# Key norms, group mean and key selection of a hybrid decoder step: three edits in one

## The chip, the cores and the metric

The kernel runs on one core of one Trainium2 chip. The metric is the device time of one execution in microseconds (us), the median of several runs. The engines of the core work in parallel, each through its own queue in order: TensorE (PE; its weight loads, PEld, overlap its matmuls), VectorE (DVE), ScalarE (ACT), GpSimd (POOL) and SyncE (SP), which issues the transfers. Matmuls write their results to PSUM, from where DVE and ACT read them.

## What is computed

One inference step of a two-layer decoder. The tokens are a prompt of 1,024 and eight sample sequences of eight tokens. Layer 0 mixes by RWKV-7 (a recurrence over a 64 x 64 state per head, 16 heads), layer 1 by sparse attention in which an indexer selects 256 keys per query; each mixer is followed by a feed-forward block (1,024 to 4,096 to 1,024). The lines of the reference that the change touches:

```python
kk = hd(k * P['rw_k_k'][j]).astype(F32)
kk = kk * lax.rsqrt(jnp.maximum(jnp.sum(kk * kk, axis=-1, keepdims=True), 1e-24))   # per token and head of 64
k = k * (1 + (a - 1) * P['rw_k_a'][j])
S, y = wkv7_scan(S0, hd(r), hd(decay), hd(k), hd(v), -kk, kk * hd(a).astype(F32))
mu = jnp.mean(y, axis=-1, keepdims=True)
var = jnp.mean(jnp.square(y - mu), axis=-1, keepdims=True)
y = ((y - mu) * lax.rsqrt(var + GN_EPS)).reshape(B, T, D)
...
adm = pos_k[None, None, :] <= pos_q[None, :, None]
_, idx = lax.top_k(jnp.where(adm, score, -jnp.inf), topk)      # topk = 256
```

## The kernel before

The tokens are worked through in two groups: A holds the 64 sample tokens and prompt tokens 0 to 511 (five token tiles, 576 columns), B holds prompt tokens 512 to 1,023 (four tiles, 512 columns). Activations lie transposed, with channels on the partitions. Large matmuls keep 32-bit accuracy by splitting weights and activations into a high and a low part (`mm3`, L133: three matmuls per block; `split`, L143; `loadw`, L113, whose high part is a cast on ScalarE).

The order in which a Python program issues the work is a priority only: when the program is built, a planner simulates the engines and lays down one fixed order per engine, in which work issued later fills the places that earlier work would leave idle, as long as its buffers are free. `RATES` (L75) says how often a step of the side work is issued between steps of the main work; where it is 0, the side work is issued after it and only fills gaps.

The stages: `rwkv_proj` (L543) of half A, with the adaLN weights streamed in beside it; the recurrence `wkv` (L945), with the projections of half B and then the output projection and feed-forward block of half A as filler; `dsa_proj` (L1002); sparse attention of A (`att_mixed`, L1359) with layer 0's feed-forward block of B as filler; sparse attention of B (`att_prompt`, L1338) with layer 1's feed-forward block of A; then what is left of A's block, and B's.

`rwkv_proj` makes six tensors; the last loop (L582 on) makes r, k and v, eight blocks of 128 channels each, and stores each block to the scratch tensor R. Its results leave PSUM through `mmt` tiles (tag o, four banks).

The recurrence is cut into 34 units (16 of half A's prompt, two of the sample group, 16 of half B), each of 256 columns: two channel blocks (a block holds two heads) by 128 tokens, or for the sample group four blocks by 64. Each unit has four parts, `prep`, `inv1`, `inv2` and `rec`; in round t the program issues, step by step in turn, `rec` of unit t-3, `inv2` of t-2, `inv1` of t-1 and `prep` of t. `prep` reads r, k, w, a, v from R, takes the key norm (`sq`, then `tokrsqrt`: matmuls that sum over the 64 channels of a head into `nps`, then `rsqrt`, L158, on 128 x 4 numbers, then matmuls that spread the root over the channels into `rb`) and makes the operands of the recurrence. `rec` runs the two chunks of 64 tokens, then the group norm of the output: mean `mu`, difference `yc`, square, and `tokrsqrt` again. All PSUM tiles of `prep` but one share one bank (tag p, `psp`), all of `rec` one other bank (tag r, `psr`), those of the inversions two (`psi`). `rsqrt` is a bit trick and three Newton steps: 11 DVE instructions in a row.

`topk` (L1171) finds the 256th largest score of each row bit by bit, from bit 30 down to bit 0 of a threshold: at each bit a candidate is made, the scores at or above it are counted, and the bit is kept or not. Bits 30 to 16 are counted on bf16 copies `tu` of the scores, the others on the scores themselves. It runs four times: in att_mixed for two prompt tiles together (384 and 512 columns) and for the 64 sample rows (2,056 columns), in att_prompt for two pairs of tiles (640 and 768, 896 and 1,024 columns).

## Time and profile before

| | us |
|---|---|
| median of three runs | 4378.32 |
| lowest and highest run | 4348.06, 4389.85 |
| profiled execution | 4376.47 |
| its span, first to last instruction | 4374.7 |
| PE busy (share) | 4008.7 (92%) |
| DVE busy | 2647.1 (61%) |
| ACT busy | 1681.9 (38%) |
| POOL busy | 971.5 (22%) |

All rows come from that one profiled execution. Busy time is time in which an instruction of the engine was running; a wait is the idle time in front of an instruction, put down to the instruction whose result came last. The granted clock is TensorE's, as a share of its higher level: 1.0 is 2.4 GHz all the time, 0.5 is 1.2 GHz all the time.

### The profile page before, as it was taken

How to read it: one execution, taken by the hardware profiler on the slowest of the kernel's cores; microseconds unless marked ns; L12 is line 12 of the kernel's file. 1: busy time of each engine (PE TensorE's matmuls, PEld its weight loads, DVE VectorE, ACT ScalarE, POOL GpSimd, SP SyncE). 2: the span in 40 equal slices, each digit the busy share in tenths (PEclk: the TensorE clock that was granted, in tenths of full speed). 3: DMA queues.
4: the chain of work that ended last, by engine and by line, in shares of the span. 5: the costliest groups of instructions: out<-in, count | busy, mean ns of one | idle time of the engine just before them, and what ended most of it. 6: DMA issues, size and time to landing. Idle time of an engine off the chain costs nothing. (4 is left out here: it accounts for less than half of the span.)

```text
span 4374.7 us, 77889 instructions
## 1 busy us (share of the span) xinstructions
PE 4008.7 (92%) x31096; PEld 3205.7 (73%) x31096; DVE 2647.1 (61%) x6822; ACT 1681.9 (38%) x3169; POOL 971.5 (22%) x762
## 2 busy tenths in 40 slices
PE   7997899998999999989899888989778999999999
PEld 5796566666777799988655565778667667998887
DVE  5513766565677655552887964442899965555444
ACT  5533544443345333332444333332443333333333
POOL 1321222222333222211111122222110000222222
PEclk7797779998798999998899999998879999999999
DMA  6675222333221122234332145444211111322332
GB/s 224 211 237 183 66 65 78 99 89 95 59 56 51 45 80 82 78 114 140 102 84 67 53 153 193 141 128 151 69 50 41 40 39 34 116 87 90 96 96 87
DMA packets 506749, 433.94 MB, mean 99 GB/s; under 512 B 93777, under 2 KB 451777, under 8 KB 501202
## 3 DMA queue, kind: packets, MB, share of 16 engines
q1 hardware_dynamic: 500498, 391.20, 30.2%
q0 software_dynamic: 5888, 37.75, 2.5%
q8 instruction: 245, 4.01, 0.4%
q14 instruction: 118, 0.97, 0.1%
HBM read 360.48 MB, written 67.87 MB: 98 GB/s over the span
## 5 line engine op out<-in xcount | busy, mean ns | idle before, releaser
L126 POOL TENSOR_TENSOR wl<-w,wh 128x1024 fp32r<-128x1024 f32 (+1 forms) x258 | 615.8, 2391 | 2330.8 <-ACT wh L122 2076.9
L140 PE MATMUL o<-hi,wh 128*128 128x512 f32 (+4 forms) x2592 | 891.8, 347 | 27.3 <-ACT hi L144 23.6
L140 PE MATMUL o<-lo,wh 128*128 128x512 f32 (+4 forms) x2592 | 890.7, 345 | 18.4 <-DVE lo L145 14.1
L140 PE MATMUL o<-hi,wl 128*128 128x512 f32 (+4 forms) x2592 | 886.3, 343 | 2.5 <-DVE wl L126 2.3
L122 ACT CAST wh<-w 128x1024 fp32r<-128x1024 f32 (+3 forms) x388 | 396.4, 1035 | 985.8 <-PE o L140 816.0
L388 DVE SCALAR_TENSOR_TENSOR xr<-o,mods,xr 128x256 f32<-128x256 f32 (+1 forms) x816 | 463.3, 570 | 292.9 <-PE o L140 281.0
L140 PEld LDWEIGHTS o<-hi,wh 128*128 128x128 f32 (+1 forms) x2592 | 499.2, 194 | 86.6 <-ACT hi L144 28.8
L140 PE MATMUL o<-uh,wh 128*128 128x320 f32 (+2 forms) x1536 | 522.1, 340 | 41.5 <-DVE xr L388 33.0
L140 PEld LDWEIGHTS o<-lo,wh 128*128 128x128 f32 (+1 forms) x2592 | 500.2, 193 | 74.2 <-DVE lo L145 20.1
L140 PEld LDWEIGHTS o<-hi,wl 128*128 128x128 f32 (+1 forms) x2592 | 499.1, 193 | 50.8 <-issue 10.0
L140 PE MATMUL o<-uh,wl 128*128 128x320 f32 (+2 forms) x1536 | 515.3, 336 | 1.8 <-POOL wl L126 1.1
L140 PE MATMUL o<-ul,wh 128*128 128x320 f32 (+2 forms) x1536 | 516.7, 336 | 0.0
L140 PEld LDWEIGHTS o<-uh,wh 128*128 128x128 f32 x1536 | 294.3, 192 | 80.3 <-DVE xr L388 41.0
L140 PEld LDWEIGHTS o<-uh,wl 128*128 128x128 f32 x1536 | 294.2, 192 | 29.8 <-issue 5.7
L140 PEld LDWEIGHTS o<-ul,wh 128*128 128x128 f32 x1536 | 294.7, 192 | 28.0 <-issue 5.8
L126 DVE TENSOR_TENSOR wl<-w,wh 128x1024 fp32r<-128x1024 f32 (+2 forms) x130 | 183.6, 1412 | 216.5 <-ACT wh L122 212.1
L145 DVE TENSOR_TENSOR ul<-z,uh 128x512 fp32r<-128x512 f32 (+1 forms) x128 | 128.5, 1004 | 164.2 <-ACT uh L144 164.1
L1018 PE MATMUL o<-wl,hi 128*128 128x256 f32 (+2 forms) x648 | 188.1, 292 | 6.9 <-POOL wl L126 6.9
L1018 PE MATMUL o<-wh,hi 128*128 128x256 f32 (+2 forms) x648 | 187.1, 291 | 6.9 <-ACT hi L144 6.9
L1018 PE MATMUL o<-wh,lo 128*128 128x256 f32 (+2 forms) x648 | 183.9, 291 | 0.0
L1268 ACT ACTIVATE sm<-sm,st 128x128 f32<-128x128 f32 (+7 forms) x128 | 99.3, 776 | 139.4 <-DVE st L1267 83.8
L1018 PEld LDWEIGHTS o<-wl,hi 128*128 128x128 f32 (+1 forms) x648 | 126.8, 196 | 9.1 <-POOL wl L126 9.1
(411 smaller groups left out, 7063.1 us busy)
## 6 DMA issues: line engine op xcount, KB each, us to landing
w<-in_w_up SPq DMA_DIRECT2D x128, 512.0 KB
w<-in_w_down SPq DMA_DIRECT2D x128, 512.0 KB
wa<-in_w_ada SPq DMA_DIRECT2D x96, 512.0 KB
w<-in_rw_w_rkv SPq DMA_DIRECT2D x48, 512.0 KB
w<-in_att_w_in SPq DMA_DIRECT2D x32, 512.0 KB
RA<-pt SPq DMA_DIRECT2D x48, 288.0 KB
RB<-pt SPq DMA_DIRECT2D x48, 256.0 KB
in<-RA SPq DMA_DIRECT2D x32, 320.0 KB
```

Of the source, the lines that this page charges most:

```text
L122: nc.scalar.copy(h[:kp, :n], w[:kp, :n])
L126: eng.tensor_tensor(out=l[:kp, :n], in0=w[:kp, :n], in1=h[:kp, :n], op=ALU.subtract)
L140: nc.tensor.matmul(o[0:M, 0:c1 - c0], a, b[:, c0:c1], start=(i == 0 and q == 0), stop=(i == n - 1 and q == 2))
L145: (lo_eng or self.nc.vector).tensor_tensor(out=lo, in0=src, in1=hi, op=ALU.subtract)
L388: nc.vector.scalar_tensor_tensor(out=xm[:, p0:c1], in0=o[:, p0 - c0:c1 - c0], scalar=self.mods[l][:, j * 8 + m, 8:9], in1=xm[:, p0:c1], op ...
L1018: nc.tensor.matmul(o[0:n, 0:cw], a, w, start=(k == 0 and q == 0), stop=(k == 7 and q == 2))
L1268: nc.scalar.activation(out=sm[:, 0:L], in_=sm[:, 0:L], func=AF.Exp, scale=-1.0, bias=mn[:, 0:1], accum_out=sums)
```

## The change

The key norm: after each block of k is stored, `rwkv_proj` squares the block (scaled by `rw_k_k`) on ScalarE, sums over each head with one matmul per token tile against a two-column selector `hsel`, and takes the maximum with 1e-24 into a small tile `kn` (128 tokens x tiles x 16 heads) that stays on the chip. After the eighth block one `rsqrt` over the whole tile (80 columns for A, 64 for B) replaces it by its root. `prep` only spreads the root of its tokens and heads into `rb`; its square, sums, maximum, `rsqrt` and one `yield` are gone. Instead of the tile that held the square, `bo` reuses `tk`.

The group mean: the matrix of `mu` is now identity minus the mean (`cent`), so its product is the difference itself; it is copied out of PSUM on ScalarE instead of being subtracted on DVE.

The selection: candidate and kept threshold are one word `cf`. Each bit is set ahead; after the count, `no` is minus the bit where the bit must be cleared, and one instruction clears it and sets the next. The bf16 copies are gone, and every count reads the 32-bit scores.

```diff
@@ -157,6 +157,9 @@
 
     def rsqrt(self, pool, x, P, n, name):
         nc = self.nc
+        if pool is None:
+            class pool:
+                tile = staticmethod(lambda shape, dt, name, tag, bufs=1: self.tmp(name, dt)[:, 0:shape[1]])
         t = pool.tile([128, n], I32, name=name + "i", tag=name + "i")
         nc.vector.tensor_scalar(out=t[:P], in0=x.bitcast(I32), scalar1=1, scalar2=None, op0=ALU.logical_shift_right)
         y = pool.tile([128, n], F32, name=name + "y", tag=name + "y", bufs=2)
@@ -181,6 +184,12 @@
         self.const = const
         self.onec = cp.tile([128, 2], F32, name="onec")
         nc.vector.memset(self.onec, 1.0)
+
+        self.hsel = cp.tile([128, 2], F32, name="hsel")
+        nc.vector.memset(self.hsel, 0.0)
+        for h in range(2):
+            nc.vector.memset(self.hsel[h * 64:h * 64 + 64, h:h + 1], 1.0)
+        self.kn = {}
 
     def vectors(self):
         nc, I, cp = self.nc, self.I, self.cp
@@ -543,6 +552,7 @@
     def rwkv_proj(self, g, h):
         nc, W, I = self.nc, g.W, self.I
         R = self.rscr(g)
+        self.kn[g.name] = self.cp.tile([128, len(g.tiles), 16], F32, name="kn" + g.name)
 
         for n, w1, w2, rk, slot in ((1, "rw_w1", "rw_w2", 64, 2), (4, "rw_a1", "rw_a2", 64, 3), (5, "rw_g1", "rw_g2", 160, 5)):
             xs = self.mixed(g, h, n)
@@ -588,6 +598,25 @@
                 self.mm3(g, [(hw[:, k * 128:k * 128 + 128], lw[:, k * 128:k * 128 + 128]) for k in range(8)], xs,
                          lambda o, c0, c1: nc.scalar.copy(t[:, c0:c1], o[:, 0:c1 - c0]))
                 nc.sync.dma_start(R[m, :, slot, 0:W], t[:, 0:W])
+                if i == 1:
+
+                    if m == 0:
+                        ss = self.kn[g.name]
+                        if g.ns:
+                            nc.vector.memset(ss[:, 0], 1.0)
+                    sq = self.tmp("ks")
+                    nc.scalar.activation(out=sq[:, 0:W], in_=t[:, 0:W], func=AF.Square, scale=self.rv["kk"][:, m:m + 1])
+                    o = self.mmt()
+                    for it, (c0, n_, _, _) in enumerate(g.tiles):
+                        nc.tensor.matmul(o[0:n_, it * 2:it * 2 + 2], sq[:, c0:c0 + n_], self.hsel, start=True, stop=True)
+                    nt = len(g.tiles)
+                    for i0, i1, P in ((0, 1, 64), (1, nt, 128)) if g.ns else ((0, nt, 128),):
+                        nc.vector.tensor_scalar(out=ss[0:P, i0:i1, m * 2:m * 2 + 2], in0=o[0:P, i0 * 2:i1 * 2].rearrange("p (i h) -> p i h", h=2),
+                                                scalar1=1e-24, scalar2=None, op0=ALU.max)
+                    if m == 7:
+                        sv = ss.rearrange("p i h -> p (i h)")
+                        y = self.rsqrt(None, sv, 128, nt * 16, "kn")
+                        nc.vector.tensor_copy(sv, y)
 
 
     def wkv_state(self):
@@ -629,23 +658,12 @@
         pps = lambda nm: self.psp.tile([128, 512], F32, name=nm, tag="p")
         ips = lambda nm: self.psi.tile([128, 512], F32, name=nm, tag="i")
 
-        def tokrsqrt(src, nm, scale, eps, mx, ps_):
-
-            ps = ps_("nps")
-            for i in range(2):
-                nc.tensor.matmul(ps[:, i * 2:i * 2 + 2], src[:, i * 128:i * 128 + 128], self.hsel, start=True, stop=True)
-            ss = T1(nm + "s", [128, 4])
-            if mx:
-                nc.vector.tensor_scalar(out=ss, in0=ps[:, 0:4], scalar1=1e-24, scalar2=None, op0=ALU.max)
-            else:
-                nc.vector.tensor_scalar(out=ss, in0=ps[:, 0:4], scalar1=scale, scalar2=eps, op0=ALU.mult, op1=ALU.add)
-            y = self.rsqrt(l1, ss, 128, 4, nm)
-            rb = ps_("rb")
-            for i in range(2):
+        def spread(y, n, ps):
+
+            for i in range(256 // n):
                 for h in range(2):
-                    nc.tensor.matmul(rb[half(h), i * 128:i * 128 + 128], y[:, i * 2 + h:i * 2 + h + 1].to_broadcast([128, 64]),
-                                     self.ident, start=True, stop=True)
-            return rb[:, 0:256]
+                    nc.tensor.matmul(ps[half(h), i * n:i * n + n], y(i)[:, h:h + 1].to_broadcast([n, 64]), self.ident[0:n, 0:n], start=True, stop=True)
+            return ps[:, 0:256]
 
         def prep():
             R = self.scr["R" + g.name]
@@ -662,11 +680,8 @@
             nc.scalar.activation(out=et(1, L + 1), in_=bst(cum), func=AF.Exp, scale=CDEC)
             Ei = T1("Ei", [128, 256])
             nc.scalar.activation(out=Ei, in_=cum, func=AF.Exp, scale=-CDEC)
-            sq = T1("sq", [128, 256])
-            for i, p in enumerate(pairs):
-                nc.scalar.activation(out=pcol(sq, i), in_=pcol(k, i), func=AF.Square, scale=rv("kk", p))
-            yield
-            rb = tokrsqrt(sq, "kn", None, None, True, pps)
+            ti = c0 // 128 if not g.ns else 0 if sam else 1 + (c0 - g.ns) // 128
+            rb = spread(lambda i: self.kn[g.name][0:tw, ti, pairs[i] * 2:pairs[i] * 2 + 2], tw, pps("rb"))
             tk = T1("tk", [128, 256])
             for i, p in enumerate(pairs):
                 nc.scalar.activation(out=pcol(tk, i), in_=pcol(a, i), func=AF.Identity, scale=rv("ka", p), bias=self.ka1[:, p:p + 1])
@@ -710,7 +725,7 @@
                 EL = X["EL"] = T3("EL", [128, 4])
                 nc.gpsimd.tensor_copy(EL, E[:, :, L])
                 nc.gpsimd.tensor_tensor(out=BH, in0=BK[:, :, 0:2], in1=EL.unsqueeze(2).unsqueeze(3).to_broadcast([128, 4, 2, 64]), op=ALU.mult)
-            bo = T1("bo", [128, 256], tag="sq")
+            bo = tk
             for i, p in enumerate(pairs):
                 nc.vector.scalar_tensor_tensor(out=pcol(bo, i), in0=pcol(r, i), scalar=rv("rk", p), in1=pcol(tk, i), op0=ALU.mult, op1=ALU.mult)
 
@@ -923,12 +938,18 @@
                     yield
 
             mu = rps("mu")
-            nc.tensor.matmul(mu[:, 0:256], self.bones, y, start=True, stop=True)
+            nc.tensor.matmul(mu[:, 0:256], self.cent, y, start=True, stop=True)
             yc = T1("yc", [128, 256])
-            nc.vector.scalar_tensor_tensor(out=yc, in0=mu[:, 0:256], scalar=-1.0 / 64, in1=y, op0=ALU.mult, op1=ALU.add)
+            nc.scalar.copy(yc, mu[:, 0:256])
             nc.scalar.activation(out=y, in_=yc, func=AF.Square)
             yield
-            rb = tokrsqrt(y, "gn", 1.0 / 64, 64e-5, False, rps)
+            ps = rps("nps")
+            for i in range(2):
+                nc.tensor.matmul(ps[:, i * 2:i * 2 + 2], y[:, i * 128:i * 128 + 128], self.hsel, start=True, stop=True)
+            ss = T1("gns", [128, 4])
+            nc.vector.tensor_scalar(out=ss, in0=ps[:, 0:4], scalar1=1.0 / 64, scalar2=64e-5, op0=ALU.mult, op1=ALU.add)
+            gy = self.rsqrt(l1, ss, 128, 4, "gn")
+            rb = spread(lambda i: gy[:, i * 2:i * 2 + 2], 128, rps("rb"))
             nc.vector.tensor_tensor(out=yc, in0=yc, in1=rb, op=ALU.mult)
             for i, p in enumerate(pairs):
                 nc.scalar.activation(out=pcol(yc, i), in_=pcol(yc, i), func=AF.Identity, scale=rv("lnw", p), bias=rv("lnb", p))
@@ -953,7 +974,9 @@
         self.bones = const("c_bones", [128, 128])
         self.smask = const("c_smask", [128, 8])
         self.rmask = const("c_rmask", [128, 2, 256], F16)
-        self.hsel = self.bones[:, 0:128:64]
+
+        self.cent = ltp.tile([128, 128], F32, name="cent")
+        self.nc.vector.scalar_tensor_tensor(out=self.cent, in0=self.bones, scalar=-1.0 / 64, in1=self.ident, op0=ALU.mult, op1=ALU.add)
 
         self.identh = ltp.tile([128, 64], F32, name="identh")
         for h in range(2):
@@ -1177,39 +1200,30 @@
             return pp.tile(shape, dt, name=nm, tag=tag, bufs=bufs)
         Lm = max(s.shape[1] for s in scs)
         cnt = T1("cnt", [128, n])[0:R]
-        m = T1("tm", [128, n], I32)[0:R]
-        cand = T1("tcand", [128, n], I32)[0:R]
         cf = T1("tcf", [128, n], I32)[0:R]
-        xm = T1("txm", [128, n], I32)[0:R]
-        ok = T1("tok", [128, n], I32)[0:R]
+        no = T1("tno", [128, n], I32)[0:R]
         junk = T1("tj", [128, Lm], BF16)[0:R]
 
-        ups = []
-        for i, s in enumerate(scs):
-            u = T1("tu%d" % i, [128, Lm], BF16)[0:R, 0:s.shape[1]]
-            nc.vector.tensor_copy(u, s.bitcast(BF16).rearrange("p (l b) -> p l b", b=2)[:, :, 1])
-            ups.append(u)
-        yield
-
-        def count(th, op, src):
-            for i, s in enumerate(src):
+        def count(th, op):
+            for i, s in enumerate(scs):
                 L = s.shape[1]
                 nc.vector.tensor_scalar(out=junk[:, 0:L], in0=s, scalar1=th if isinstance(th, float) else th[:, i:i + 1], scalar2=None,
                                         op0=op, op1=ALU.add, accum_out=cnt[:, i:i + 1])
-        count(0.0, ALU.is_ge, scs)
-        nc.vector.tensor_scalar(out=xm, in0=cnt, scalar1=float(TOPK) - 0.5, scalar2=-1.0, op0=ALU.is_lt, op1=ALU.mult)
-        nc.vector.memset(m, 0)
+        count(0.0, ALU.is_ge)
+
+        nc.vector.tensor_scalar(out=no, in0=cnt, scalar1=float(TOPK) - 0.5, scalar2=-1.0, op0=ALU.is_lt, op1=ALU.mult)
+        nc.vector.tensor_scalar(out=cf, in0=no, scalar1=1 << 30, scalar2=None, op0=ALU.bitwise_xor)
+        th = cf.bitcast(F32)
         yield
         for b in range(30, -1, -1):
-            nc.vector.tensor_scalar(out=cand, in0=m, scalar1=1 << b, scalar2=None, op0=ALU.bitwise_or)
-            nc.vector.tensor_tensor(out=cf, in0=cand, in1=xm, op=ALU.bitwise_xor)
-            count(cf.bitcast(F32), ALU.is_ge, ups if b >= 16 else scs)
-            nc.vector.tensor_scalar(out=ok, in0=cnt, scalar1=float(TOPK) - 0.5, scalar2=None, op0=ALU.is_ge)
-            nc.vector.copy_predicated(m, ok, cand)
-            yield
-        nc.vector.tensor_tensor(out=cf, in0=m, in1=xm, op=ALU.bitwise_xor)
-        th = cf.bitcast(F32)
-        count(th, ALU.is_gt, scs)
+            count(th, ALU.is_ge)
+            nc.vector.tensor_scalar(out=no, in0=cnt, scalar1=float(TOPK) - 0.5, scalar2=float(1 << b), op0=ALU.is_lt, op1=ALU.mult)
+            if b:
+                nc.vector.scalar_tensor_tensor(out=cf, in0=no, scalar=1 << (b - 1), in1=cf, op0=ALU.bitwise_xor, op1=ALU.bitwise_xor)
+            else:
+                nc.vector.tensor_tensor(out=cf, in0=no, in1=cf, op=ALU.bitwise_xor)
+            yield
+        count(th, ALU.is_gt)
         yield
         for i, s in enumerate(scs):
             L = s.shape[1]
@@ -1403,7 +1417,7 @@
                 p2, p3 = P("attt", 1, c1), P("attsi", 1, c1)
                 ssc = p3.tile([64, LS], F32, name="ssc")
                 tiles = [None] + [self.att_tile(g, i, p2, S[i], 512) for i in range(1, 5)]
-                smp = [self.sample_index(p3, ssc, gather, ki_rows, csm), self.topk(p3, [ssc], 64, {"tj": ("kis", 1), "tu0": ("rls", 1), "teq": ("kiraw", 2), "trk": ("kiraw", 2)},
+                smp = [self.sample_index(p3, ssc, gather, ki_rows, csm), self.topk(p3, [ssc], 64, {"tj": ("kis", 1), "teq": ("kiraw", 2), "trk": ("kiraw", 2)},
                                                                                                    lambda s: [s[:, a * 1024:a * 1024 + 1024].rearrange("r (b c) -> r c b", b=2)[:, c0:c0 + 256]
                                                                                                               for a in range(2) for c0 in (0, 256)] + [s[:, PAST:LS].unsqueeze(2)])]
                 self.together(RATES["tile1A"], [self.topk(p2, S[3:5], place={"teq": ("sm", 3), "trk": ("sm", 3)})], tiles[1:3], smp[0:1])
```

## Rows read from the trace of the kernel before

**Rows 1.** The page: busy us (share of the span) and instructions of each engine.

```profile
PE 4008.7 (92%) x31096; PEld 3205.7 (73%) x31096; DVE 2647.1 (61%) x6822; ACT 1681.9 (38%) x3169; POOL 971.5 (22%) x762
```

**Rows 2.** By stage: start:end us, length, PE, PEld, DVE, ACT, POOL busy, clock, DMA.

```profile
0.00:392.00 392.00, 354.06 (x2594) 286.88 (x2594) 148.40 (x300) 172.52 (x326) 91.41 (x53) 0.85 0.73 229
392.00:1040.00 648.00, 589.45 (x5836) 402.67 (x5834) 408.44 (x1181) 296.99 (x653) 172.68 (x208) 0.83 0.30 83
1040.00:1570.00 530.00, 497.50 (x6624) 398.58 (x6625) 364.94 (x1251) 220.68 (x533) 164.20 (x204) 0.89 0.20 56
...
2180.00:2540.00 360.00, 323.94 (x1561) 205.39 (x1561) 312.38 (x820) 145.72 (x321) 57.07 (x33) 0.94 0.25 69
...
3080.00:3520.00 440.00, 370.88 (x2159) 292.40 (x2157) 402.79 (x1164) 157.11 (x299) 42.62 (x19) 0.86 0.17 50
```

**Rows 3.** Waits of PE, 392 to 1570: line, releaser, total us, times, longest.

```profile
PE spn L918 <- DVE S L912: 8.1, 12, 2.0
...
PE rb L646 <- DVE kny L170: 6.1, 5, 2.5
...
PE nps L636 <- DVE BT L728: 4.0, 4, 2.0
...
PE bb L732 <- DVE UV L728: 0.6, 1, 0.6
```

**Rows 4.** Waits of PE on DVE, first and last: 2180 to 2540, then 3080 to 3520.

```profile
PE o L140 <- DVE xr L388: 9.2, 2, 8.6
PE sp L1169 <- DVE tok L1207: 5.3, 3, 2.7
...
PE il L1440 <- DVE kis L1435: 0.2, 1, 0.2
...
PE pt L1285 <- DVE PT L1287: 12.4, 9, 4.9
...
PE sp L1169 <- DVE ql L1163: 0.4, 1, 0.4
```

**Rows 5.** Timeline of PE: start us, length, line, output, inputs, count.

```profile
498.61 0.61 PE L636 MATMUL nps<-c_bones,sq 128*128 128x2 f32 x4
...
528.35 0.61 PE L636 MATMUL nps<-c_bones,y 128*128 128x2 f32 x4
...
531.40 0.61 PE L636 MATMUL nps<-c_bones,sq 128*128 128x2 f32 x4
...
535.01 0.66 PE L646 MATMUL rb<-c_ident,gny 128*64 128x128 f32 x8 [0.79 <-DVE gny L170]
...
537.39 1.11 PE L646 MATMUL rb<-c_ident,kny 128*64 128x128 f32 x6
```

**Rows 6.** Groups of instructions, whole span: count, busy us, mean ns, idle before.

```profile
L170 DVE SCALAR_TENSOR_TENSOR kny<-knb,kny 128x4 f32<-128x4 f32 x102 | 26.3, 258 | 1.6
...
L636 PE MATMUL nps<-c_bones,sq 128*128 128x2 f32 x136 | 22.2, 265 | 4.1 <-DVE BT L728 4.0
...
L257 ACT COPY adas<-oa 128x256 f32<-128x256 f32 x48 | 17.9, 373 | 45.8 <-PE oa L255 45.8
...
L928 DVE SCALAR_TENSOR_TENSOR yc<-mu,y 128x256 f32<-128x256 f32 x34 | 14.4, 424 | 21.5 <-PE mu L926 19.9 <-PE o L140 1.5
```

**Rows 7.** Timeline of DVE in the selection of half B, one bit.

```profile
3271.45 0.17 DVE L1207 TENSOR_SCALAR tok<-cnt 128x2 int32<-128x2 f32 x1
...
3272.25 0.88 DVE L1197 TENSOR_SCALAR_CACHE_REDUCE tj<-sc,tcf 128x640 bf16<-128x640 f32 x1
```

**Rows 8.** The selection's counts by form: shortest, middle and longest ns.

```profile
L1197 DVE TENSOR_SCALAR_CACHE_REDUCE tj<-tu,tcf x105: 579/1005/2346, 2196.6 to 3409.1; 128x384 bf16<-128x384 bf16 x15, 128x512 bf16<-128x512 bf16 x15, 64x2056 bf16<-64x2056 bf16 x15, 128x640 bf16<-128x640 bf16 x15
...
L1197 DVE TENSOR_SCALAR_CACHE_REDUCE tj<-sc,tcf x102: 598/944/1280, 2252.8 to 3510.7; 128x384 bf16<-128x384 f32 x17, 128x512 bf16<-128x512 f32 x17, 128x640 bf16<-128x640 f32 x17, 128x768 bf16<-128x768 f32 x17
...
L1197 DVE TENSOR_SCALAR_CACHE_REDUCE tj<-ssc,tcf x17: 2335/2346/2349, 2457.7 to 2524.9; 64x2056 bf16<-64x2056 f32 x17
```

**Rows 9.** Waits of ACT, 392 to 1570.

```profile
ACT wh L122 <- PE o L140: 46.1, 30, 8.9
```

## Prediction, made before the changed kernel ran

> **What bounds the kernel now.** I read the page's busy shares first [rows 1]: TensorE (PE) is busy 4,008.7 of 4,374.7 us, so in the whole run it stands idle for only 366 us. No other engine is near that. A change of about 1% must therefore either take work off PE or close some of those idle stretches.
>
> Next the busy time by stage [rows 2], in which the reader should look at the two columns PE and DVE. In the first 392 us (projections of half A with the adaLN weights; granted clock 0.85 on average) PE is busy 354 us. In the recurrence (392 to 1,570 us) PE is busy 589.5 of 648 and 497.5 of 530 us, so 91 us idle, with VectorE (DVE) at 63% and 69%; the recurrence's small matmuls and the big matmuls that the builder lays between them fill PE together. In the two attention stages that hold the key selection the picture turns: DVE is busy 312 of 360 us (PE idle 36 us) and 403 of 440 us (PE idle 69 us). There DVE is nearly the bound.
>
> Third the waits of PE: in the recurrence 21 of its rows name DVE, 8.1 us down to 0.6 us, 70 us in all [rows 3]. The key norm's own rows among them are 6.1 us (spread matmuls waiting for the root) and 4.0 us (the sums). In the attention stages 12 rows of 9.2 to 0.2 us name DVE in A, 33 us in all, and 9 rows of 12.4 to 0.4 us in B, 57 us in all [rows 4].
>
> Last, one round of the recurrence [rows 5]. From the key norm's sum matmul of one unit to that of the next is 32.8 us (498.61 to 531.40), and from the sum to the spread matmul 6.0 us (531.40 to 537.39). All of prep's PSUM goes through one bank (tag p, bufs 1), so these 6 us sit in prep's serial chain. The output norm's chain of the unit three rounds older runs at the same time (528.35 to 535.01, 6.7 us), its small DVE instructions taking turns with the key norm's.
>
> **The change part by part.** The profiled execution took 4,376.5 us (span 4,374.7), 1.8 us below the median of the three runs, 4,378.3; I sum against 4,376.5.
>
> *Key sums moved into the projections.* Per unit two matmuls, each two PE instructions, go: 34 units x 4 = 136, 22.2 us of PE, 0.163 us each [rows 6]. Added are 8 blocks x 5 token tiles x 2 = 80 in A and 8 x 4 x 2 = 64 in B. A's fall into the first 392 us, where 354 us are busy and the later half is denser: 80 x 0.163 = **+13 us** (bounds 0, if the 38 idle us take them, and 80 x 0.265 = 21 us at the row's mean length). B's, 10 us, fall among the recurrence's filler: there -22 + 10 = **-12 us** (bounds -22 and 0). Nothing is issued to SP or POOL by the moved step. The new squares go to ScalarE (16 instead of 72), which is idle 56% of stage one. Each block holds one of the four PSUM banks of tag o until DVE has taken the maximum; I price that at nothing, since the next block's 48 matmuls and the adaLN stream stand behind it; without that cover, 16 blocks x about 1 us (estimate: two copies like the 0.37 us one in [rows 6] and a short DVE instruction) = 16 us. The two roots over 80 and 64 columns, 11 DVE instructions each and a copy, are hidden under the third projection: no unit can begin before its values arrive. The constants are set once, off the path.
>
> *Key root out of the unit.* Twelve DVE instructions per unit go, 408 in all. The three largest groups of the root have 102 each; the one shown is 26.3 us, 0.258 us each with its stalls [rows 6]. At 0.2 us (the pace of a lone chain, [rows 7]) to 0.258 us that is 82 to 105 us of DVE. With the 14.4 us of the mean's subtraction, and about 10 us added back, DVE drops by some 90 to 110 of 773 us. What it gives PE lies between the waits that name the chain itself, 6.1 + 4.0 = 10 us, and all 70 us of waits on DVE. I take **-25 us**: the 10 whole, and 15 of the other 60, because the output norm no longer takes turns with the key norm (6.7 us now; alone twelve steps of 0.2 us would be 2.4 us), while the state's own hops stay.
>
> *Group mean on PE.* The matmul keeps its size. A DVE instruction of 424 ns becomes a ScalarE copy out of PSUM; the nearest row, same shape, is 373 ns [rows 6]: 34 x 0.373 = 12.7 us on ScalarE, which is 46% and 42% busy there. On the path 34 x (0.424 - 0.373) = 2 us less, taken as nothing. Behind that copy on ScalarE stands the square, which needs it anyhow; the next recurrence matmul waits for the bank.
>
> *One-word selection.* Per bit four small DVE instructions become two. In a lone chain they start 0.2 us apart (3271.45, four of them, the count at 3272.25) [rows 7]; 62 bits per stage x 2 x 0.2 = 25 us of DVE per stage, and the seven copies to bf16 go, so some 28 us per stage (the copies' 3 us an estimate: three or four per stage, each one pass like the counts of [rows 8], some of them shorter). The counts now read 32-bit words for all bits. Their rows at the same shapes: 579 ns shortest and 2,346 ns longest from bf16, 598 and 2,346 ns from 32-bit words [rows 8]: no price.
>
> The Trainium skill speaks against this edit: "VectorE: DVE Perf Modes", section "The perf-mode tier table", lets a single-source instruction run at twice the rate on bf16 in SBUF (693 against 1,227 ns for 2,048 columns). By that, an estimate: 0.26 ns per column more for 15 bits and the 6,280 columns of the seven score rows would add some 25 us of DVE and eat half of the gain. The rows above don't agree, and I go by them.
>
> PE can win no more than its waits. In B, 28 us of DVE against 57 us of waits, DVE 92% busy: I take **-20 us** (bounds 0 and -28). In A, PE is 90% busy and only 13 us of waits name the selection's small instructions (the largest is in [rows 4]): **-10 us** (bounds 0 and -28). Big matmuls that found room in a stage and no longer do run later, so only idle time is a gain.
>
> Sum: 13 - 12 - 25 - 10 - 20 = -54, so 4,376.5 - 54 = 4,322.5, and about 4,324 against the median.
>
> **The rivals.** *PE was full anyway.* The edits do what they say, but only the waits that name them go: 13 - 12 - 10 = -9 us, 4,369 against the median. For it: PE is busy 91 to 94% of the recurrence. Against it: the DVE-bound stages.
>
> *The chains were the bound.* Prep's round of 32.8 us loses 6, the output norm some 3; over 34 units at least 100 us, more than PE has idle, so all waits on DVE go: 13 - 12 - 70 - 28 - 28 = -125, 4,253 against the median. Against it: waits on DVE that come from other DVE work.
>
> *The copy gets stuck on ScalarE (slower).* ScalarE works in its order, and its queue holds weight casts that wait for PE to free a buffer: 30 waits, 46.1 us, up to 8.9 us in the recurrence [rows 9]. A copy placed behind one keeps the recurrence's only PSUM bank (tag r). It decides from (4,378.3 x 1.01 - 4,324) / 34 = 2.9 us per unit; with 3.3 us the time is 4,324 + 112 = 4,436. Against it: the mean wait is 1.5 us (34 x 1.5 = 51 us, about no change), and the square stood in that same queue before.
>
> *Counts from words are slower.* If every count that read bf16 took twice as long, 105 x 1,005 ns (the middle row) = 106 us would be added to nearly full DVE stages: up to 4,430. The rows speak against it. This is the page's rule as a mechanism, at its strongest.
>
> **How the numbers follow.** Forecast 0.52 (own range 4,295 to 4,355), PE full 0.24, chains 0.13, stuck copy 0.09, slower counts 0.02. The prediction is 4,324 us. About 1%, 44 us, is what a measurement of this kernel can tell from no change, so faster begins below 4,334.5: 0.34 of the forecast's 0.52 and the 0.13 give 0.47; same is the rest of it, 0.18, and 0.24: 0.42; slower is 0.11. The range runs from the chains' case, 4,253, to the upper bounds of the terms, 21 + 0 - 10 = +11 and thus 4,389 against the median; it leaves out the slower cases and half of the chains' case, about 0.18.
>
> **What would show it.** After the change: 144 sum matmuls of the keys in the projections and none in the units; stage one longer by 10 to 20 us; the recurrence shorter by some 37 us with PE idle near 65 us instead of 91; prep's round with no 6 us between sum and spread; the output norm's chain nearer 4 than 6.7 us; the selection at two small instructions per bit and unchanged count lengths; PE idle in stage B near 50 us. The prediction is wrong if PE's idle time in the recurrence stays, if the granted clock of a stage falls, or if the copy after the mean starts microseconds after its matmul.

## The result, and the profile after

| | before | after |
|---|---|---|
| median, us | 4,378.47 (4 runs, 4,348.06 to 4,389.85) | 4,314.32 (4 runs, 4,312.25 to 4,326.98) |
| profiled execution, us | 4,376.47 | 4,326.98 |
| its mean granted clock | 0.912 | 0.911 |

The ratio is 0.9863, 95% interval 0.9831 to 0.9895: faster by 1.4%. A second measurement of the same kernel, beside the experiments below, gave 0.9825 (0.9771 to 0.988). Between the two profiled executions, whose clocks are alike, the gain is 49.5 us; the sum in the prediction was 54. All ratios and means here leave out three executions of one kernel below (the mean alone: 4,384.5 to 4,399.3 us, clock 0.906 to 0.911), which counted as slow.

The page's busy line, which answers to [rows 1]: DVE has lost 126 us and 648 instructions, PE 15 us.

```profile
PE 3993.6 (92%) x31120; PEld 3206.4 (74%) x31120; DVE 2521.2 (58%) x6174; ACT 1681.0 (39%) x3147; POOL 969.0 (22%) x762
```

To compare stages I cut both executions at the same events: the last copy of the adaLN stream, the last spread of the output norm, the first decision of half A's selection, the last indexer result of A stored, the last projection of half B, the first tie ranking of B's last tile (the end of its selection), the end. The busy time in these seven stretches (columns as in [rows 2]: start:end, length, busy time and instructions of PE, PEld, DVE, ACT, POOL, granted clock, DMA share, GB/s), of the kernel before and then of after:

```profile
0.00:391.90 391.90, 353.96 (x2593) 286.81 (x2594) 148.30 (x300) 172.42 (x326) 91.41 (x53) 0.85 0.73 229
391.90:1557.50 1165.60, 1075.55 (x12372) 790.32 (x12372) 765.75 (x2410) 513.35 (x1177) 331.82 (x406) 0.86 0.25 71
1557.50:2193.20 635.70, 583.21 (x4058) 553.15 (x4055) 344.32 (x822) 213.07 (x340) 138.86 (x67) 0.94 0.34 101
2193.20:2556.50 363.30, 324.31 (x1557) 206.04 (x1557) 316.57 (x828) 139.25 (x308) 53.09 (x31) 0.93 0.24 66
2556.50:3036.40 479.90, 436.32 (x3356) 347.36 (x3354) 195.02 (x326) 168.28 (x236) 124.42 (x109) 0.95 0.50 158
3036.40:3521.30 484.90, 406.56 (x2361) 322.88 (x2361) 438.86 (x1249) 177.72 (x342) 49.02 (x23) 0.86 0.20 58
3521.30:4374.70 853.40, 828.75 (x4810) 699.13 (x4808) 438.24 (x897) 297.80 (x442) 182.87 (x75) 0.99 0.27 82
```

```profile
0.00:410.20 410.20, 371.72 (x2673) 300.20 (x2674) 151.95 (x332) 177.21 (x332) 91.20 (x53) 0.83 0.68 218
410.20:1540.50 1130.30, 1049.49 (x12287) 776.54 (x12286) 678.94 (x1988) 506.96 (x1146) 325.85 (x405) 0.86 0.25 72
1540.50:2189.00 648.50, 596.01 (x4089) 564.07 (x4085) 347.87 (x818) 214.96 (x345) 141.27 (x68) 0.93 0.33 100
2189.00:2520.30 331.30, 299.46 (x1500) 192.23 (x1499) 285.18 (x693) 135.43 (x304) 53.25 (x30) 0.96 0.24 68
2520.30:3006.30 486.00, 447.04 (x3413) 355.68 (x3411) 196.91 (x332) 170.40 (x240) 123.66 (x109) 0.96 0.49 159
3006.30:3452.50 446.20, 378.39 (x2189) 296.73 (x2190) 405.23 (x1093) 169.70 (x330) 43.30 (x20) 0.86 0.19 58
3452.50:4325.00 872.50, 851.50 (x4980) 720.97 (x4979) 455.16 (x925) 306.30 (x454) 190.44 (x78) 0.99 0.27 83
```

Read the lengths first, and then distrust them. Stage one is 18 us longer, the recurrence 35 shorter, selection A (fourth line) 32 and selection B (sixth) 39 shorter. But the stretches behind them are longer, by 13, 6 and 19 us, since PE's instruction count moved with them: B's selection holds 172 matmuls fewer, the last stretch 170 more. Matmuls that had filled a DVE-bound stage run later when the stage is short. What is left after that shift is PE's idle time, length minus busy, summed over stretches: up to the first count (lines one to three) 180.5 us before and 171.8 after; behind it 185.6 before and 159.6 after. The rest is PE's busy time: behind the first count 1,995.9 us before and 1,976.4 after, for as many matmuls, and up to it 2,012.7 before and 2,017.2 after. So the 49.7 us between the two spans are 8.7 + 26.0 us of idle time, 19.5 us of busy time behind the first count, and -4.5 us in front of it.

### The profile page after: what moved, and what is told of

It is laid out like the page before. It is cut to its first block, busy times and chain, and to the rows that moved or that the text cites. A ratio compares the mean times of both kernels' runs of the same rounds, so it can differ in the third digit from the quotient of the medians.

```text
span 4325.0 us, 77351 instructions
## 1 busy us (share of the span) xinstructions
PE 3993.6 (92%) x31120; PEld 3206.4 (74%) x31120; DVE 2521.2 (58%) x6174; ACT 1681.0 (39%) x3147; POOL 969.0 (22%) x762
## 5 line engine op out<-in xcount | busy, mean ns | idle before, releaser
L1210 DVE TENSOR_SCALAR_CACHE_REDUCE tj<-sc,tcf 128x384 bf16<-128x384 f32 (+2 forms) x192 | 180.4, 939 | 2.4
```

The lines of the kernel that those rows point to most:

```text
L1210: nc.vector.tensor_scalar(out=junk[:, 0:L], in0=s, scalar1=th if isinstance(th, float) else th[:, i:i + 1], scalar2=None, op0=op, op1=ALU. ...
```

## Two measures for all the experiments

Single executions of one kernel differ by 15 to 64 us (lowest to highest), and the difference follows the mean granted clock that each execution lists: through all 149 executions of the kernels below, each kernel with its own mean, an execution is 3.3 us shorter for each 0.001 of clock, with 3 us of scatter left. So I give beside each ratio the kernel's mean time moved along that line to a clock of 0.911, that of the profile after; the two separate measurements of the changed kernel agree there at 4,330.1 and 4,330.4. The second measure is PE's idle time in the profile, up to the first count and behind it, and PE's busy time behind it, worked out from the same seven stretches.

| kernel | ratio (95%) | mean clock | us at 0.911 | PE idle to first count | idle behind | busy behind |
|---|---|---|---|---|---|---|
| before | 1 | 0.910 | 4,381.6 | 180.5 | 185.6 | 1,995.9 |
| key norm alone | 0.997 (0.9948 to 0.9991) | 0.909 | 4,359.7 | 180.3 | 185.3 | 1,995.2 |
| mean alone | 0.9949 (0.9918 to 0.998) | 0.916 | 4,377.5 | 178.4 | 186.8 | 1,991.3 |
| selection alone | 0.9895 (0.9858 to 0.9932) | 0.914 | 4,346.6 | 177.4 | 160.2 | 1,975.2 |
| all but key norm | 0.9893 (0.9866 to 0.992) | 0.914 | 4,343.9 | 177.5 | 156.7 | 1,977.4 |
| all but mean | 0.9884 (0.986 to 0.9908) | 0.913 | 4,327.5 | 180.1 | 159.2 | 1,975.0 |
| all but selection | 0.9951 (0.992 to 0.9982) | 0.911 | 4,365.7 | 173.4 | 187.0 | 2,005.6 |
| all | 0.9863 (0.9831 to 0.9895) | 0.915 | 4,330.1 | 171.8 | 159.6 | 1,976.4 |
| all, again | 0.9825 (0.9771 to 0.988) | 0.918 | 4,330.4 | 172.8 | 161.1 | 1,971.2 |

The mean clock is itself not the same for all kernels, and the table can't say whether an edit moves it. So "us at 0.911" tells apart two kernels of like clock; where clocks differ the ratio is the measured fact. If an edit does move the clock, the column takes that part of its worth away; experiment 4 shows that this is likely for the selection.

## Experiment 1: each edit alone

Each kernel is the kernel before with one part of the change, taken over unaltered; for the mean, for instance:

```diff
-            nc.tensor.matmul(mu[:, 0:256], self.bones, y, start=True, stop=True)
+            nc.tensor.matmul(mu[:, 0:256], self.cent, y, start=True, stop=True)
...
-            nc.vector.scalar_tensor_tensor(out=yc, in0=mu[:, 0:256], scalar=-1.0 / 64, in1=y, op0=ALU.mult, op1=ALU.add)
+            nc.scalar.copy(yc, mu[:, 0:256])
```

> The kernel before with the key norm alone moved into the projections (mean and selection as before). Theory (the sum of terms): stage one about 15 us longer, the recurrence about 30 to 35 us shorter, so 4,378 - 15 to - 20, a ratio of 0.995 to 0.997. Rival (PE was full anyway): the recurrence gives back only what stage one costs, within 5 us of before. Rival (the chains were the bound): 40 us or more, below 0.991. The two attention stages keep their lengths.

> The kernel before with the one-word selection alone. Theory: two small DVE instructions per bit and the bf16 copies gone, 28 us of DVE in each of the two attention stages; net 30 to 40 us, ratio 0.991 to 0.993, the selection of the sample rows some 20 us shorter from its first count to its result, recurrence unchanged. Rival (counts from 32-bit words are slower): no gain or a loss of up to 50 us, the counts of the upper bits longer than before.

> The kernel before with the group mean taken off by PE and copied on ScalarE alone. Theory: 34 times 0.05 us, no change within 5 us. Rival (the copy gets stuck on ScalarE behind weight casts): 1.5 to 3 us per unit, 50 to 100 us longer, ratio 1.01 to 1.02, and the copy starts microseconds behind its matmul.

Measured: the three lines of the table. At one clock the selection is worth 35 us, the key norm 22 and the mean 4. The key norm alone leaves PE's idle time where it was, 180.3 against 180.5 us, and so does the mean (178.4). The selection alone brings the whole change of idle time behind the first count (185.6 to 160.2). The mean's ratio looks better than its 4 us because its executions had a clock of 0.916.

Of the expectations, the key norm's ratio came out as its theory said (0.997, the upper end of 0.995 to 0.997), though the waits that the theory counted on did not shrink. The selection's ratio, 0.9895, is a little better than the 0.991 to 0.993 expected, within its interval. The mean's ratio, 0.9949, is outside the 5 us expected; only at one clock does it fit.

Where the key norm's time lies if PE's idle time stays shows in PE's busy time up to the first count, of the kernel before and of the key norm alone:

```profile
0.00:2193.20 2193.20, 2012.72 (x19017) 1630.28 (x19018) 1258.37 (x3531) 898.84 (x1842) 562.08 (x526) 0.88 0.36 108
0.00:2174.90 2174.90, 1994.62 (x19041) 1631.43 (x19042) 1197.15 (x3175) 890.43 (x1786) 556.54 (x526) 0.88 0.36 108
```

PE is busy 18 us less at a like clock, though it runs 24 matmuls more. Which of its overlapping matmuls became cheaper no run separates; in the changed kernel the same column is 2,017.2 and 1,998.0 us in two profiles, at clocks of 0.875 and 0.885.

## Experiment 2: the change with one edit undone

These are the changed kernel with one part as it was before (for the selection the old `topk` with its bf16 copies; for the key norm `tokrsqrt` and the square back in `prep`; for the mean the lines above, the other way).

> The changed kernel with the old selection. Theory: the selection carries most of the change, so 30 to 45 us of the 60 go: 4,345 to 4,360, ratio 0.994 to 0.997. Rival (the recurrence carries it): 4,325 to 4,335, ratio 0.988 to 0.991.

> The changed kernel with the key norm back in every unit. Theory (terms): 13 to 20 us slower than the changed kernel, ratio 0.990 to 0.991. Rival (the key norm's move pays in stage one what it saves later): the same as the changed kernel, ratio 0.985 to 0.988.

> The changed kernel with the group mean back on DVE. If the mean's edit alone is worth the 0.5% that it gave on the kernel before, by its work (a hop less between engines in each unit), this is about 20 us slower than the changed kernel: 4,335, ratio 0.991. If that gain came from the order drawn anew (order alone moved the time by 16 us the other way), it need not show here: within 10 us of the changed kernel or even below it, ratio 0.984 to 0.989.

Measured at one clock, against 4,330: the selection is worth 36 us, the key norm 14, the mean -3 (nothing). That agrees with the edits alone (35, 22, 4), whose sum, 61, is above the whole change's 51. The 8 us of idle time up to the first count need the key norm and the mean together: 171.8 to 173.4 us in the kernels of the table with both, 177 to 181 us in those with one or none. The ratios say the same of the selection (0.9951, as its theory had it) and of the mean (0.9884, that its gain need not show here); the key norm's, 0.9893, lies between its theory and the rival.

## Experiment 3: the order alone

The old key norm has a `yield` behind its square; the new one has none there. Here the kernel before loses that `yield` and nothing else, so that its planner draws another order of the same instructions:

```diff
                 nc.scalar.activation(out=pcol(sq, i), in_=pcol(k, i), func=AF.Square, scale=rv("kk", p))
-            yield
             rb = tokrsqrt(sq, "kn", None, None, True, pps)
```

> The kernel before with one step boundary taken out of prep (the one that the key norm's move also removes): the same instructions, only their priorities shift, so the builder draws another order. If the gain of the change comes from its terms, this moves less than 10 us. Rival (the order drawn anew is what moves the time): 20 us or more, of either sign.

Measured: ratio 1.0037 (1.0014 to 1.006), 4,393 us at 0.911, PE idle 201.9 us up to the first count instead of 180.5. That is 16 us by the ratio, between the expectation's 10 and its rival's 20. An order drawn anew is worth 12 us of time and 21 us of idle time here, nearly all of it in the recurrence. So the 8 us above, and the key norm's 14 and 22 us, may in part be a drawn order. The changed kernel has no `yield` there either, so this kernel, and not the one before, has its step boundaries; the section on the prediction comes back to that.

## Experiment 4: what in the selection gained

Two edits were made in one: two small instructions fewer per bit, and no bf16 copies (with the counts on words for all bits). The first kernel puts the copies back and keeps the one-word chain:

```diff
+        ups = []
+        for i, s in enumerate(scs):
+            u = T1("tu%d" % i, [128, Lm], BF16)[0:R, 0:s.shape[1]]
+            nc.vector.tensor_copy(u, s.bitcast(BF16).rearrange("p (l b) -> p l b", b=2)[:, :, 1])
+            ups.append(u)
...
-            count(th, ALU.is_ge)
+            count(th, ALU.is_ge, ups if b >= 16 else scs)
```

> The changed kernel with its one-word selection, but bits 30 to 16 counted on bf16 copies again, as before the change. If counts cost the same from bf16 and from 32-bit words, the copies are the only difference: 0 to 8 us slower than the changed kernel, ratio 0.986 to 0.989, and the counts of equal shape last equally long. If bf16 counts are faster (the perf-mode rule), the DVE-bound stages shorten and this is up to 25 us faster, ratio 0.981 to 0.984.

The second keeps the words and pads the chain to four small instructions per bit:

```diff
             nc.vector.tensor_scalar(out=no, in0=cnt, scalar1=float(TOPK) - 0.5, scalar2=float(1 << b), op0=ALU.is_lt, op1=ALU.mult)
+            for _ in range(2):
+                nc.vector.tensor_scalar(out=no, in0=no, scalar1=1.0, scalar2=None, op0=ALU.mult)
```

> The changed kernel with two more small VectorE instructions per bit of the selection (a word multiplied by 1, twice, in the chain between compare and new threshold), so four per bit as before, but no copies to bf16 and one word format. If the selection gained by its small instructions (62 bits x 2 x 0.2 us a stage), stage A grows from 331 us and stage B from 446 us by 20 to 28 us each, towards the 363 and 484 us of the old selection. If it gained by the copies left out, the buffer that they held or the counts, each grows by less than 8 us.

> The changed kernel again, beside the three kernels above. If its gain rests on work taken away, the ratio is within 0.983 to 0.990 again, at a granted clock near that of the kernel before. If part of it is the clock that its executions happened to get (0.915 against 0.910 on average), executions at 0.911 take about 4,330 us.

| kernel | ratio (95%) | mean clock | us at 0.911 | idle behind first count | busy behind |
|---|---|---|---|---|---|
| with bf16 copies | 0.9902 (0.987 to 0.9933) | 0.912 | 4,341.6 | 162.5 | 1,991.7 |
| padded chain | 0.9843 (0.9799 to 0.9887) | 0.919 | 4,348.3 | 175.3 | 1,975.3 |
| all (two measurements) | 0.9863 and 0.9825 | 0.915, 0.918 | 4,330 | 159.6, 161.1 | 1,976.4, 1,971.2 |

The stretches from the first count on, of the padded kernel:

```profile
2181.30:2545.80 364.50, 325.67 (x1603) 211.84 (x1602) 318.34 (x828) 144.59 (x314) 58.70 (x32) 0.95 0.25 69
2545.80:3006.90 461.10, 424.61 (x3310) 336.81 (x3308) 189.75 (x322) 163.82 (x230) 118.40 (x107) 0.95 0.51 162
3006.90:3498.10 491.20, 413.65 (x2464) 332.03 (x2464) 448.79 (x1267) 181.23 (x349) 53.42 (x25) 0.88 0.20 60
3498.10:4331.80 833.70, 811.32 (x4705) 682.39 (x4704) 434.01 (x873) 292.21 (x435) 177.65 (x73) 1.00 0.27 82
```

The small instructions alone set the lengths of the two selection stages: padded, A is 364.5 us and B 491.2, as long as in the kernel before (363.3 and 484.9), and DVE's busy time is back at 318 and 449 us. Yet the next stretches are 25 and 39 us shorter than in the changed kernel, as they have 103 and 275 matmuls less to do. What stays is 16 us of PE's idle time, of the 26 that the selection edit took. At one clock it costs 18 us; by its ratio it can't be told from the changed kernel at all, since its executions had a clock of 0.919. So of this run's two theories the first is right; the stages grew by 33 and 45 us, more than the 20 to 28 that it gave to each, but only a part of that length is time of the whole.

The copies act on something else. With them the idle time hardly moves (162.5), but PE's busy time behind the first count is 1,991.7 us again, and at one clock the kernel takes 11 us more than the changed one, above the 0 to 8 expected. In all fourteen profiles that busy time falls into two groups without overlap: 1,991 to 2,006 us in the five with the old selection and this one, 1,971 to 1,980 us in the eight without copies. Behind the first count, one line each for the kernel before, with copies, after, padded:

```profile
2193.20:4374.70 2181.50, 1995.93 (x12080) 1575.41 (x12079) 1388.69 (x3294) 783.05 (x1327) 409.40 (x237) 0.94 0.30 91
2181.60:4335.80 2154.20, 1991.73 (x12077) 1572.92 (x12077) 1339.49 (x3043) 783.30 (x1327) 411.13 (x236) 0.94 0.30 92
2189.00:4325.00 2136.00, 1976.38 (x12079) 1565.61 (x12077) 1342.48 (x3038) 781.83 (x1327) 410.65 (x236) 0.95 0.30 93
2181.30:4331.80 2150.50, 1975.24 (x12079) 1563.07 (x12077) 1390.90 (x3286) 781.85 (x1327) 408.17 (x236) 0.95 0.30 92
```

The column behind POOL's is the granted clock, and it has the same two groups: to three places 0.939 to 0.946 in the six profiles with copies, 0.948 to 0.954 in the eight without. The clock is at its lower level (1.2 GHz) for 236 to 268 us of this stretch with copies and 196 to 221 us without. If the busy time at that level is counted half, PE's work behind the first count is 1,899 to 1,905 us in all fourteen, whatever the group (worked out from the clock records of the traces). So the matmuls didn't get cheaper: they ran more of their time at 2.4 GHz. Up to the first count the clocks of the two groups overlap (0.875 to 0.883 with copies, 0.862 to 0.885 without). Over all executions the mean clock is 0.9108 with copies (107 executions) and 0.9138 without (42), about 10 us at 3.3 us for each 0.001. The selection's 35 us "at 0.911" leave those out; by its ratio it is worth 46 us. Why copies of 6.5 us of DVE in all, and the buffers that they hold, go with a lower clock is not shown; it stays open.

The counts themselves cost the same from both formats. Shape by shape, within the kernel with copies, the medians from bf16 and from 32-bit words differ by at most 4 ns (1,006 and 1,006.5 at 128 x 768). The lines below each mix several shapes; the middle figure is the median in ns, first of the kernel with copies, then after:

```profile
L1216 DVE TENSOR_SCALAR_CACHE_REDUCE tj<-tu,tcf x105: 594/1006/2346, 2184.9 to 3345.8; 128x384 bf16<-128x384 bf16 x15, 128x512 bf16<-128x512 bf16 x15, 64x2056 bf16<-64x2056 bf16 x15, 128x640 bf16<-128x640 bf16 x15
```

```profile
L1210 DVE TENSOR_SCALAR_CACHE_REDUCE tj<-sc,tcf x192: 574/936/1280, 2191.6 to 3441.2; 128x384 bf16<-128x384 f32 x32, 128x512 bf16<-128x512 f32 x32, 128x640 bf16<-128x640 f32 x32, 128x768 bf16<-128x768 f32 x32
...
L1210 DVE TENSOR_SCALAR_CACHE_REDUCE tj<-ssc,tcf x32: 2323/2342/2347, 2361.0 to 2491.3; 64x2056 bf16<-64x2056 f32 x32
```

## Experiment 5: what the key sums cost in the projections

Every sum matmul of the squares is issued twice, the second over the first:

```diff
                     for it, (c0, n_, _, _) in enumerate(g.tiles):
-                        nc.tensor.matmul(o[0:n_, it * 2:it * 2 + 2], sq[:, c0:c0 + n_], self.hsel, start=True, stop=True)
+                        for _ in range(2):
+                            nc.tensor.matmul(o[0:n_, it * 2:it * 2 + 2], sq[:, c0:c0 + n_], self.hsel, start=True, stop=True)
```

> The changed kernel with every sum matmul of the key squares in the projections issued twice (the second overwrites the first; 80 more in half A, 64 more in half B). If stage one grew by the matmuls themselves (80 x 0.16 to 0.25 us), it grows by a further 13 to 20 us over the changed kernel's 410 us, and half B's projections by about 10 to 16 us of filler, some 20 to 30 us in all. If it grew by something else (the PSUM bank that the sums hold, the roots, another order of the work), stage one stays within 5 us of 410 us and the whole within 10 us of the changed kernel.

Measured: ratio 0.9918 (0.9888 to 0.9949); at one clock 4,350, 20 us more than the changed kernel. Stage one is a further 17 us longer, with 80 matmuls more:

```profile
0.00:427.20 427.20, 387.31 (x2753) 317.07 (x2754) 151.94 (x332) 177.08 (x332) 91.16 (x53) 0.82 0.66 210
```

20 us for 144 matmuls is 0.14 us each, near the prediction's 0.163; the group of all sums is busy 40.7 us instead of 20.8. Both figures are in the ranges of the first theory (13 to 20 us in stage one, 20 to 30 in all): the moved sums are paid on PE's path.

## Experiment 6: does a lighter VectorE help the recurrence?

A root of 12 small DVE instructions is put back into each unit's `prep`, with the finished norms as its input; nobody reads its result:

```diff
+            kx = T1("kds", [128, 4])
+            nc.vector.tensor_scalar(out=kx, in0=self.kn[g.name][:, ti, pairs[0] * 2:pairs[0] * 2 + 4], scalar1=1e-24, scalar2=None, op0=ALU.max)
+            self.rsqrt(l1, kx, 128, 4, "kd")
             rb = spread(lambda i: self.kn[g.name][0:tw, ti, pairs[i] * 2:pairs[i] * 2 + 2], tw, pps("rb"))
```

> The changed kernel with a root of 12 small VectorE instructions put back into each unit of the recurrence, for whose result nobody waits (its input is the finished key norms). VectorE has the old load back, the path from sum to spread does not. If the recurrence gained because VectorE does less, it grows from 1,130 us by 15 us or more, towards the 1,175 us of the kernel that keeps the key norm in its units. If it gained because the unit's chain lost the sum, the root and the PSUM bank between them, it stays within 8 us of 1,130 us.

Measured: ratio 0.9925 (0.9891 to 0.9958), 4,351 us at one clock, 21 us more than the changed kernel. The recurrence is 1,168 us long, which looks like the first theory. It isn't a test of it, though: the planner put the roots where their input was ready, not into the units. The roots' first instruction, shortest, middle and longest ns, first and last start:

```profile
L685 DVE TENSOR_SCALAR kds<-knA x18: 160/163/2396, 335.5 to 384.0; 128x4 f32<-128x4 f32 x18
L685 DVE TENSOR_SCALAR kds<-knB x16: 157/163/165, 1075.5 to 1129.6; 128x4 f32<-128x4 f32 x16
```

All 34 run in two bursts, and there PE stands idle. By stretch, first this kernel around its bursts, then the changed kernel around the same events:

```profile
335.00:420.00 85.00, 73.22 (x562) 62.91 (x561) 50.51 (x241) 19.09 (x40) 11.03 (x10) 0.86 0.60 189
1070.00:1140.00 70.00, 55.43 (x251) 44.51 (x252) 61.49 (x235) 26.05 (x44) 15.87 (x12) 0.84 0.51 156
```

```profile
328.00:412.00 84.00, 79.06 (x639) 68.02 (x637) 11.41 (x37) 21.59 (x45) 13.07 (x10) 0.92 0.68 215
1036.00:1083.00 47.00, 46.18 (x208) 37.82 (x208) 16.56 (x30) 21.85 (x34) 13.13 (x7) 0.96 0.65 197
```

PE is idle 11.8 and 14.6 us in them, against 4.9 and 0.8; over the whole kernel its idle time is 191.3 us up to the first count (171.8) and 156.4 behind it (159.6). In the second burst PE's longest waits name DVE work behind it, 8.0 us for `S` and 4.3 for `wl`. In the first they name the transfers of the adaLN weights (10.1 us, against 3.1), so that the burst is to blame there is likely, not shown. The rest of the recurrence's length in this profile is a clock of 0.83 in it, against 0.86. So 408 small DVE instructions that nobody waits for came with some 20 us of PE's idle time in two bursts, but whether the same load spread over the units costs PE anything is left open by this run. The key norm alone, which takes it away, has the idle time of the kernel before (180.3 us against 180.5), but it has lost the `yield` of experiment 3 too.

## The prediction, point by point

**The total was right for partly wrong reasons.** 4,324 was forecast, 4,314 measured, inside the likeliest case's own range; 54 us of gain against 49.5 between the profiled executions. But the sum put 24 us of it before the first count (13 - 12 - 25) and 30 behind it; measured at one clock it is 14 to 22 us for the key norm, about nothing for the mean, and 35 for the selection. Between the profiled executions only 34.7 us are idle time; the other 15 are PE's busy time, for which the sum had +1 us. That so much of it made up for the recurrence is luck.

**Key sums in the projections, +13 us and -12 us: right in size, with a wait left out.** Stage one grew by 18.3 us, 9.4 us in the second profile of the changed kernel, whose clock in it was 0.87 instead of 0.83; twice the sums cost another 17. In the recurrence PE's busy time fell by 26 us with 85 matmuls fewer, and rose by 12.8 with 31 more in the stretch behind it: 13 us net, as forecast; in the other profiles with the moved norm (without the two of experiments 5 and 6) this net is 9 to 35 us, so that its closeness is in part chance. In stage one PE's idle time stayed (37.9 us before, 38.5 after), and none of its waits there names the maximum that frees the sums' PSUM bank. In half A, PE stood idle 0.2 us in front of the sums themselves; in half B, in the recurrence, it waited 6.7 us for their squares on ScalarE, for which the sum has no term (each line from its own stretch of the kernel after):

```profile
L611 PE MATMUL o<-hsel,ks 128*128 128x2 f32 (+1 forms) x80 | 10.1, 244 | 0.2
...
L611 PE MATMUL o<-hsel,ks 128*128 128x2 f32 x64 | 10.8, 290 | 6.7 <-ACT ks L608 6.7
```

**Recurrence waits, -25 us: the step that failed.** PE's idle time in the recurrence went from 90.1 to 80.8 us (79.9 in the second profile), not to 65, and with the key norm alone it is 87.0. The two rows that name the key norm in [rows 3] are indeed gone, 10.1 us. In their place, PE's waits in the changed recurrence (line, releaser, us in total, times, longest):

```profile
PE gp L712 <- DVE BK L701: 14.6, 12, 3.8
PE o L611 <- ACT ks L608: 6.7, 5, 2.1
...
PE rb L665 <- DVE gny L173: 4.7, 7, 2.2
```

The first row was 3.4 us before, the second is the moved squares. `prep`'s serial chain did get shorter: from one unit's key spread to the next the middle gap is 22.6 us, 26.7 before (the round of 32.8 us in the prediction was a long one). But `BK`, a product further down in the same chain, is late instead, by as much as the two rows that went.

The run of the order alone bears on why. It has the old key norm and lacks only the `yield`, and there `BK` is late already. Its row, and its recurrence, then that of the key norm alone:

```profile
PE gp L696 <- DVE BK L685: 13.2, 17, 2.2
...
390.70:1567.60 1176.90, 1068.09 (x12351) 786.35 (x12351) 751.16 (x2409) 516.30 (x1176) 330.01 (x406) 0.85 0.25 70
411.00:1533.20 1122.20, 1035.16 (x12286) 772.75 (x12286) 697.78 (x2021) 497.90 (x1111) 323.62 (x405) 0.86 0.25 73
```

PE is idle 108.8 us in the one and 87.0 in the other. Against the kernel with the same step boundaries the moved norm thus takes 22 us of idle time, nearly the 25; against the kernel before it takes 3. What the prediction left out is the step boundary that goes with the norm: it has no term for the order drawn anew, and that order comes with the late `BK` and some 20 us. As far as these runs show, that ate the term. A changed kernel with the `yield` put back would decide it; there is no such run, so the cause stays open.

The output norm's chain, from its sum matmul to its spread, was to come nearer to 4 us once it no longer took turns with the key norm; over the units its middle value went from 6.9 to 6.2 us only, and the round that answers to [rows 5] shows 6.4:

```profile
544.00 0.61 PE L948 MATMUL nps<-hsel,y 128*128 128x2 f32 x4
...
550.42 0.66 PE L665 MATMUL rb<-c_ident,gny 128*64 128x128 f32 x8
```

**Group mean, nothing: right.** At one clock it is worth 4 us alone and -3 within the change. The rival of the stuck copy fell: the copy starts 0.09 us behind its matmul (middle of 34; 1.3 us at most), and its duration is that of the row taken for it in [rows 6], 373 ns:

```profile
L943 ACT COPY yc<-mu 128x256 f32<-128x256 f32 x34 | 12.7, 372 | 17.1 <-PE mu L941 16.8
```

**Selection, -10 and -20 us: the right place, mis-sized as a whole.** The chain has two small instructions per bit. In this one of half B's selection, on DVE's timeline, the next count starts 0.67 us after the compare, with two instructions of the filler among them (0.8 us in [rows 7], with four of the chain):

```profile
3203.35 0.16 DVE L1220 TENSOR_SCALAR tno<-cnt 128x2 int32<-128x2 f32 x1
...
3203.81 0.15 DVE L1222 SCALAR_TENSOR_TENSOR tcf<-tno,tcf 128x2 int32<-128x2 int32 x1
...
3204.02 0.87 DVE L1210 TENSOR_SCALAR_CACHE_REDUCE tj<-sc,tcf 128x640 bf16<-128x640 f32 x1
```

PE's idle time behind the first count fell by 26 us, close to the 30 taken: 7.2 in A, 10.5 in B (not 20) and 8.3 in the two stretches behind them, which the prediction didn't count. The row of [rows 4] with 12.4 us in B is down to 4.2, and a wait on other DVE work, a norm of the feed-forward block (`acc`), is new. Of PE's waits in the changed kernel's stage B:

```profile
PE o L338 <- DVE acc L333: 6.6, 1, 6.6
...
PE pt L1299 <- DVE PT L1301: 4.2, 5, 2.0
```

On top of it came what the prediction had no term for, some 20 us less of PE's busy time for the same matmuls: the granted clock behind the first count was higher (0.949 against 0.943), as in all profiles without the bf16 copies. "Only idle time is a gain" held for PE's work and left out its clock.

**Slower counts from words: fell.** 2,342 ns from 32-bit words and 2,346 from bf16 at 64 x 2,056. The doubled rate that the Trainium skill ("VectorE: DVE Perf Modes", section "The perf-mode tier table") lets a bf16 source have isn't seen in this form of instruction, one that also adds up its result; the measurement decides.

**What would have made it wrong** occurred in part. The granted clock of the recurrence was 0.86 in both; stage one's fell from 0.85 to 0.83 in this profile and was 0.87 in the second. PE's idle time in the recurrence stayed nearly as it was, which the prediction had named as a sign against it. The total came out right in spite of that, since PE's busy time behind the first count fell by the clock there.

## What to carry to other kernels

When filler work flows between stages, a stage's length says little: add up the bound engine's idle time and busy time over all the stages behind an edit, as the padded chain shows (two stages 33 and 45 us longer, 16 us of idle time). When a move also takes out a step boundary, run the boundary alone: here it cost as much idle time as the move was to save. Compare kernels at one granted clock, or with enough executions, before a difference below 1% is read as an edit's, and look at the clock by stretch: one that differs in every profile with the edit may belong to the edit.

## What the runs showed of the hardware that was not expected

- The mean granted clock explains nearly all scatter between executions of one kernel: 3.3 us for each 0.001, with 3 us left. The clocks of one kernel's executions scatter by 0.003 to 0.006 (standard deviation), which is 0.2 to 0.4% of the time.
- PE's busy time behind the first count, for the same matmuls, was 1% lower in every profile without the bf16 copies, and the granted clock was at 1.2 GHz there for 196 to 221 us, against 236 to 268 with copies. Why the copies go with it is open.
- The same instructions in another order cost 0.37% (0.14 to 0.6%).
- Counts with an added-up result took the same from bf16 and from 32-bit words, to 4 ns in the median of each of seven shapes.
